# Dense expert layer with choice weights: pacing of the building stretch, place of the weights' second parts, and the buffers of the last activations

## The chip, the cores and the metric

The kernel runs on 1 core of one Trainium2 chip. The metric is device time in microseconds (us), from the first to the last instruction with the launch around it. TensorE (PE), VectorE (DVE), ScalarE (ACT), GpSimd (POOL) and SyncE (SP) each run their own instructions in order and wait for each other by semaphores; DMA transfers are issued from the SP, ACT and POOL queues.

## The reference

Two transformer blocks for 512 tokens of width 1024. The change lies in the expert layer of the first block (PEER), which chooses 16 of 16384 one-neuron experts per token and head:

```python
q = (xb @ wq).reshape(PEER_BLOCK, PEER_HEADS, 2, PEER_DKEY // 2)
s1 = jnp.einsum('thd,hnd->thn', q[:, :, 0], keys[:, 0])
s2 = jnp.einsum('thd,hnd->thn', q[:, :, 1], keys[:, 1])
v1, i1 = lax.top_k(s1, PEER_TOPK)          # the same for s2
...
e = i1[ci // 16] * PEER_NKEYS + i2[ci % 16]
g = jax.nn.softmax(sc, axis=-1)
hid = jnp.einsum('thkd,td->thk', u[e], xb)
a = jax.nn.gelu(hid, approximate=False) * g
return jnp.einsum('thk,thkd->td', a, v[e])
```

Everything is float32.

## The kernel before

Matrix products are made of three float32r products: a weight tile `raw` is split into a first part `whi` (ACT copies and rounds it, L147) and a second part `wlo` (DVE subtracts, L149), and `mm_segs` multiplies both by the first part of the activations (L71, L72) and `whi` by their second part (L76).

The expert layer treats its first 128 tokens by gathered rows and the other 384 densely. **Dense part, first half:** for all 128 groups of 128 experts, `G = gelu(U x)` is computed by `hidden(i)`, a unit of two groups. A unit has two pieces (weight tiles of 512 KB, `raw<-in_peer_u`); a piece has four row tiles, each of six 384-column matmuls, so 24 matmuls. The Gelu (L1262) of a unit comes in the next unit's first step; its result goes from tile `G` (2 buffers) to DRAM (`Gd`, issued on ACT's queue). `wget` splits weights two pieces ahead: at the start of piece i it issues `whi` and `wlo` of piece i+2, with 3 buffers each.

**Beside it runs a side stream**, which `pace` mixes with the units: a unit is cut into `PARTS` main steps, and after each the side stream is given a share of time in units of a written cost table. It holds

- the *choice*: `topk_block` for four blocks of 128 tokens (DVE's max, match and index operations, POOL multiplications);
- the *building* of the dense choice weights A in six chunks of 64 tokens, 16 build steps each. A step issues on DVE the one-hots `o2` (L1212) and `o1` (L1215) of two steps ahead, on ACT four scalings of `o2` (L1214, `hot<-hot`), on PE four matmuls into `aps` (L1232; two PSUM buffers), and on ACT the copy of the step before into `ab` (L1235); `ab` goes to DRAM (`Ad`) by 16 writes, issued one per later step from ACT, those of the last chunk from POOL (L1287) after the side stream;
- the *rows*: for the first 128 tokens, `rg.step` gathers 128 rows of U by an indirect DMA (POOL, L1019, 4 row buffers) and reduces them on DVE (L1028). `UH` = 120 of them are due before the side stream ends, of which `UT` during the choice.

From the start of the building on, DVE and ACT run in the order in which the code is written (`manual_schedule`); PE, POOL and SP are ordered by a scheduler. `N1` groups lie beside the side stream; the units that are left (`i >= N1 // 2`) follow it alone. Then comes the **second half** (peer_v): for each group DVE multiplies `gt` (its G) by `at` (its part of A, read back from `Ad`, L1308), ACT and DVE split the product, and 24 matmuls (L55, L56, L58) accumulate into eight PSUM tiles that `rg.empty` has cleared by eight 512-column matmuls with a zero tile `rz` (L1052, L1054). The second half begins with the last four groups, whose G (units 62 and 63) never goes to DRAM: in the kernel before their Gelu writes tiles `gt` of the pool `lp`, which is opened after the building's pools are closed and takes their memory.

Of the kernel before, what the change touches and what calls it, by code (L numbers as in the profile page):

```python
# [9 lines left out]
F32 = mybir.dt.float32  # L10
F32R = mybir.dt.float32r
# [7 lines left out]
P = 128  # L19
# [26 lines left out]
def r32(ap):  # L46
    return ap.bitcast(F32)
# [17 lines left out]
def mm_segs(nc, x, items, start, stop):  # L65

    xh, xl = x
    for s in range(len(items[0][0])):
        sl = items[0][0][s][1]
        for segs, (lh, ll) in items:  # L70
            nc.tensor.matmul(segs[s][0], lh, xh[:, sl], start=start, stop=False)  # L71
            nc.tensor.matmul(segs[s][0], ll, xh[:, sl], start=False, stop=False)  # L72
    for s in range(len(items[0][0])):
        sl = items[0][0][s][1]
        for segs, (lh, _) in items:
            nc.tensor.matmul(segs[s][0], lh, xl[:, sl], start=False, stop=stop)  # L76


def setup(tc, es, A):
    g = Ctx()  # L80
    nc = tc.nc
    g.tc, g.nc, g.A = tc, nc, A
    g.const = es.enter_context(tc.tile_pool(name="const", bufs=1))
    g.res = es.enter_context(tc.tile_pool(name="res", bufs=1))
    g.wp = es.enter_context(tc.tile_pool(name="wp", bufs=3))
    g.np_ = es.enter_context(tc.tile_pool(name="np", bufs=2))
    c = g.const

    def cin(name, shape, now=True):
        t = c.tile(shape, F32, name="c_" + name)  # L90
        if now:
            nc.sync.dma_start(t, A[name])
        return t

    g.cin = cin
    g.vec = cin("vecs", [P, NVEC])
    g.ident = cin("ident", [P, P], False)
    g.ones = c.tile([P, P], F32, name="ones")
    nc.gpsimd.memset(g.ones, 1.0)
    g.eps = c.tile([P, 1], F32, name="eps")  # L100
    nc.gpsimd.memset(g.eps, EPS)
    g.zero = c.tile([P, 1], F32, name="zero")
    nc.gpsimd.memset(g.zero, 0.0)
    g.pre = {}
    g.raw = {}
    g.nraw, g.third = 0, None
    g.queue = []
    g.h = [None] * KT
    h_tiles(g)
    return g  # L110


def h_tiles(g):
    for k in range(KT):
        g.h[k] = g.res.tile([P, T], F32, tag=f"h{k}", name=f"h{k}")
# [23 lines left out]
    return raw  # L139


def wload(g, raw, pool, hl):

    nc = g.nc
    _, a, b = raw.shape
    hi = pool.tile([P, a, b], F32R, tag="whi", name="whi", bufs=hl)
    nc.scalar.activation(hi, raw, AF.Copy)  # L147
    lo = pool.tile([P, a, b], F32R, tag="wlo", name="wlo", bufs=hl)
    nc.vector.tensor_tensor(lo, raw, r32(hi), op=ALU.subtract)  # L149
    return hi, lo  # L150


def wstart(g, name, *idx):

    key = (name, idx)
    if key not in g.raw and key not in g.pre:
        g.raw[key] = wraw(g, wsrc(g, name, idx))


def wpre(g, name, *idx):  # L160

    key = (name, idx)
    if key not in g.pre:
        wstart(g, name, *idx)
        g.pre[key] = wload(g, g.raw.pop(key), g.wp, 3)


def wget(g, name, *idx):

    key = (name, *idx)  # L170
    wpre(g, *key)
    if key in g.queue[:1]:
        g.queue.pop(0)
        for k in g.queue[:2]:
            wpre(g, *k)
        for k in g.queue[2:3 if g.third is None else 4]:
            wstart(g, *k)
    return g.pre.pop((name, idx))


def gemm_fm(g, segs, name, ct, rhs):
# [10 lines left out]
def gemm2(g, accs, name, ct, rhs, out=None, pieces=None):  # L192

    keys = keys2(g, name, ct, pieces)
    for i, key in enumerate(keys):
        hi, lo = wget(g, *key)
        for k in range(4):
            ws = [(hi[:, k, e * P:(e + 1) * P], lo[:, k, e * P:(e + 1) * P]) for e in range(2)]
            mm_segs(g.nc, rhs(4 * i + k), list(zip(accs, ws)), i == 0 and k == 0, i == len(keys) - 1 and k == 3)
            yield 1.3  # L200
    if out is not None:
        out()
# [734 lines left out]
NK = 128  # L937
# [2 lines left out]
LAST = 3  # L940

AHEAD_V = 2
N1 = 122
PARTS = 4


GT = 128
# [5 lines left out]
CH = 64  # L953
NCK = ND // CH

UH, UT = 120, 44

T16, T256, TLK, BUILD, ROW = 2.2, 3.1, 2.0, 1.3, 1.4
TOPKS = 16 * T16 + 3 + 8 * T256 + 8 * TLK + 2
# [101 lines left out]
def peer_block(g, ni, tail):  # L1061

    tc, nc, A = g.tc, g.nc, g.A
    with ExitStack() as es:
# [14 lines left out]
        with ExitStack() as e1:  # L1079
# [161 lines left out]
                for i in range(0, NK, n):  # L1241
                    out.append((Ad[c, :, i:i + n], buf[:, i:i + n]))

            def hidden(i, ts=None):

                at = {}

                def step(p):
                    if p == 0:
                        at["acc"] = [acc.get(ND) for _ in range(2)]  # L1250
                        at["gen"] = gemm2(g, [a[0] for a in at["acc"]], "peer_u", i, X)
                    for _ in range(8 // PARTS):
                        next(at["gen"])
                    if p == 0 and ends:
                        ends.pop(0)()
                    if p == PARTS - 1:
                        ends.append(end)

                def end():
                    gt = gp.tile([P, 2, ND], F32, tag="G", name="G") if ts is None else ts  # L1260
                    for e in range(2):
                        nc.scalar.activation(gt[:, e], at["acc"][e][1], AF.Gelu)  # L1262
                    if ts is None:
                        nc.scalar.dma_start(Gd[i], gt)
                return [(lambda p=p: step(p)) for p in range(PARTS)]

            ends = []
            chosen, picked = {}, {}
            out = []

            def weights():

                for b in range(4):
                    for n, c in enumerate(topk_block(b)):
                        yield c
                        if n == 12 and GT < b * P:
                            chosen[b - 1] = tokens_last(b - 1)
                for _ in range(8):
                    yield 1.0
                chosen[3] = tokens_last(3)  # L1280
                order_kept.append(kept.enter_context(tc.manual_schedule(engines={mybir.EngineType.DVE, mybir.EngineType.Activation})))
                e2.close()
                ab = e1.enter_context(tc.tile_pool(name="p_ab", bufs=2))
                for c in range(NCK):
                    yield from build(ab, c)
                while out:
                    tc.keep_in_program_order(nc.gpsimd.dma_start(*out.pop(0)))  # L1287
# [23 lines left out]
        def two_in(i):  # L1311

            gt = lp.tile([P, 2, ND], F32, tag="gt", name="gt", bufs=3)
            if i < NK - FIRST:
                tc.keep_in_program_order(nc.scalar.dma_start(gt, Gd[i // 2]))
            return gt


        ats, gts = {}, {}

        def expert(n):
            i = order[n]
# [16 lines left out]
            return lo  # L1339

        ats[NK - FIRST] = four_in(NK - FIRST)
        for i in range(NK - FIRST, NK, 2):
            gts[i] = two_in(i)

        for i in range(N1 // 2, NK // 2):
            for m in hidden(i, gts.get(2 * i)):
                m()
        while ends:
            ends.pop(0)()
        h_tiles(g)  # L1350
        tail.load(es)
        accs = [pp.tile([P, 512], F32, name=f"acc{k}") for k in range(3)] + [acc.get()[1] for _ in range(5)]
# [923 lines left out]
```

## Time and profile before

| | |
|---|---|
| device time, median of 3 runs | 3642.78 us (3641.7 to 3643.01) |
| the profiled execution's own time | 3628.02 us |
| its span | 3626.3 us |
| PE busy in the span | 3483.1 us (96%) |
| DVE busy | 2399.4 us (66%) |
| ACT busy | 1591.4 us (44%) |
| POOL busy | 776.2 us (21%) |
| mean granted TensorE clock | 0.981 |

The profile is of one execution. Matmuls are pipelined, so PE's busy time overstates its work; what is read below is mostly idle time ahead of an instruction, with what ended it. In rows of the trace, a line is that of the kernel before, "x" counts instructions, and a bracket gives the idle time of the engine just before and the releaser.

### The profile page before, as it was taken

The numbers are of one execution on the slowest core, as the hardware profiler recorded it, in microseconds if no ns is written. First come the engines' busy times: TensorE is split into PE (matmuls) and PEld (weight loads), VectorE is DVE, ScalarE is ACT, GpSimd is POOL, SyncE is SP. The second block draws the span as 40 slices with busy tenths as digits, with TensorE's granted clock in tenths as the row PEclk, the third lists the DMA queues.
The fourth block names the chain that finished last, engine by engine and source line by source line (L and its number), as shares of the span: only waits on it lengthen the run. The fifth ranks groups of instructions, "written<-read, shape, count | busy, mean of one in ns | idle before, by whom it ended". The sixth has DMA issues, their size and how long they took to land. (4 is left out here: it accounts for less than half of the span.)

```text
span 3626.3 us, 56462 instructions
## 1 busy us (share of the span) xinstructions
PE 3483.1 (96%) x21979; PEld 3164.9 (87%) x21979; DVE 2399.4 (66%) x4395; ACT 1591.4 (44%) x2998; POOL 776.2 (21%) x828
## 2 busy tenths in 40 slices
PE   8999999999898889999999999999999999999999
PEld 6777888898887779999998899999899998878887
DVE  5764457999967658888887677767643345564433
ACT  4555333333477763333346444445422235343222
POOL 2421010333322232333332322222100003120000
PEclk9999999999999999999998999999999999999999
DMA  4233233566678889999972121111132322213222
GB/s 134 76 88 88 82 124 122 198 225 221 233 237 279 270 299 369 358 360 353 363 257 77 56 63 57 47 52 52 48 98 90 94 88 83 75 59 99 93 93 93
DMA packets 169492, 557.60 MB, mean 154 GB/s; under 512 B 19617, under 2 KB 20130, under 8 KB 169224
## 3 DMA queue, kind: packets, MB, share of 16 engines
q1 hardware_dynamic: 90228, 313.50, 26.1%
q0 software_dynamic: 49136, 170.64, 14.2%
q10 hardware_dynamic: 29860, 69.84, 5.3%
q8 instruction: 173, 2.83, 0.3%
q14 instruction: 95, 0.78, 0.1%
HBM read 492.20 MB, written 55.41 MB: 151 GB/s over the span
## 5 line engine op out<-in xcount | busy, mean ns | idle before, releaser
L72 PE MATMUL ps<-xh,wlo 128*128 128x264 f32 (+2 forms) x3296 | 1051.3, 331 | 45.0 <-DVE wlo L149 44.8
L71 PE MATMUL ps<-xh,whi 128*128 128x264 f32 (+2 forms) x3296 | 1069.6, 337 | 18.8 <-ACT xh L288 13.5
L149 DVE TENSOR_TENSOR wlo<-raw,whi 128x1024 fp32r<-128x1024 f32 x562 | 718.6, 1279 | 531.2 <-ACT whi L147 524.8
L147 ACT ACTIVATE whi<-raw 128x1024 fp32r<-128x1024 f32 x562 | 594.5, 1058 | 978.9 <-PE ps L76 782.6
L76 PE MATMUL ps<-xl,whi 128*128 128x264 f32 (+2 forms) x3296 | 813.1, 331 | 6.5 <-DVE xl L289 6.4
L72 PEld LDWEIGHTS ps<-xh,wlo 128*128 128x128 f32 x3296 | 629.6, 192 | 91.5 <-DVE wlo L149 61.4
L71 PEld LDWEIGHTS ps<-xh,whi 128*128 128x128 f32 x3296 | 630.2, 192 | 59.3 <-ACT xh L288 15.9
L76 PEld LDWEIGHTS ps<-xl,whi 128*128 128x128 f32 x3296 | 563.6, 192 | 39.3 <-DVE xl L289 8.9
L1019 POOL DMA_INDIRECT row<-in_peer_ur_dram,rix x128 | 146.1, 1142 | 465.7 <-DVE row L1028 372.1
L71 PE MATMUL ps<-ah,whi 128*128 128x264 f32 (+1 forms) x768 | 230.1, 320 | 0.0
L72 PE MATMUL ps<-ah,wlo 128*128 128x264 f32 (+1 forms) x768 | 229.9, 320 | 0.0
L55 PE MATMUL ps<-ah,whi 128*128 128x384 f32 x640 | 215.5, 337 | 0.0
L56 PE MATMUL ps<-ah,wlo 128*128 128x384 f32 x640 | 215.1, 336 | 0.0
L1019 POOL DMA_INDIRECT row<-in_peer_v_dram,rix x128 | 138.1, 1079 | 276.9 <-DVE ro L1032 261.5
L280 POOL TENSOR_TENSOR ssum<-ssum,sq 128x512 f32<-128x512 f32 (+1 forms) x49 | 75.1, 1538 | 460.4 <-ACT sq L279 459.8
L1028 DVE SCALAR_TENSOR_TENSOR row<-row,rx 128x1024 f32<-128x1024 f32 x128 | 164.0, 1283 | 6.2 <-DMA row<-in_peer_ur_dram,rix 6.2
L1333 ACT ACTIVATE ah<-gt 128x384 fp32r<-128x384 f32 x128 | 67.3, 526 | 227.4 <-DVE gt L1331 227.4
L76 PE MATMUL ps<-al,whi 128*128 128x264 f32 (+1 forms) x768 | 163.2, 321 | 0.0
L1214 ACT ACTIVATE hot<-hot,lt 128x128 f32<-128x128 f32 x384 | 122.0, 390 | 93.3 <-DVE hot L1212 89.6
L1032 DVE SCALAR_TENSOR_TENSOR ro<-row,rhid,ro 128x1024 f32<-128x1024 f32 x127 | 162.4, 1278 | 0.6 <-DMA row<-in_peer_v_dram,rix 0.4
L71 PEld LDWEIGHTS ps<-ah,whi 128*128 128x128 f32 x768 | 144.3, 188 | 11.4
L72 PEld LDWEIGHTS ps<-ah,wlo 128*128 128x128 f32 x768 | 144.3, 188 | 10.9
(429 smaller groups left out, 6184.7 us busy)
## 6 DMA issues: line engine op xcount, KB each, us to landing
raw<-in_peer_u_dram SPq DMA_DIRECT2D x128, 512.0 KB, 5.5
raw<-in_peer_v_dram SPq DMA_DIRECT2D x128, 512.0 KB, 6.9
raw<-in_ff_up_dram SPq DMA_DIRECT2D x64, 512.0 KB, 3.4
raw<-in_ff_down_dram SPq DMA_DIRECT2D x64, 512.0 KB, 3.5
at<-Ad POOLq DMA_DIRECT2D x32, 768.0 KB, 7.2
raw<-in_gdn_in_dram SPq DMA_DIRECT2D x48, 512.0 KB, 3.5
Gd<-G ACTq DMA_DIRECT2D x62, 384.0 KB, 3.2
gt<-Gd ACTq DMA_DIRECT2D x62, 384.0 KB, 5.2
```

The lines of the kernel that those rows point to most:

```text
L55: nc.tensor.matmul(out, lh, rh, start=start, stop=False)
L56: nc.tensor.matmul(out, ll, rh, start=False, stop=False)
L71: nc.tensor.matmul(segs[s][0], lh, xh[:, sl], start=start, stop=False)
L72: nc.tensor.matmul(segs[s][0], ll, xh[:, sl], start=False, stop=False)
L76: nc.tensor.matmul(segs[s][0], lh, xl[:, sl], start=False, stop=stop)
L147: nc.scalar.activation(hi, raw, AF.Copy)
L149: nc.vector.tensor_tensor(lo, raw, r32(hi), op=ALU.subtract)
L280: g.nc.gpsimd.tensor_tensor(self.t[:, 0:n], self.t[:, 0:n], sq[:, 0:n], op=ALU.add)
L1019: nc.gpsimd.indirect_dma_start(out=t, out_offset=None, in_=(self.U, self.V)[e], in_offset=bass.IndirectOffsetOnAxis(ap=self.ix[:, j:j + 1] ...
L1028: o = nc.vector.scalar_tensor_tensor(t, t, 1.0, self.x, op0=ALU.mult, op1=ALU.mult, accum_out=a)
L1032: o = nc.vector.scalar_tensor_tensor(self.o, t, a, self.o, op0=ALU.mult, op1=ALU.add)
L1214: nc.scalar.activation(oh[:, j], o2[:, j], AF.Copy, scale=lt[:, 2, 4 * t4 + j:4 * t4 + j + 1])
```

## The change

Five edits. (1) From the start of the building to the end of the first half (`g.late`), `wload` returns a function that makes `wlo`; `gemm2` calls it after the matmuls of the first row tile of the piece that is being multiplied. (2) `PARTS` 4 to 8: a main step is one row tile, not two, and the side stream's share per step is halved. (3) `N1` 122 to 118: ten groups (five units) are left behind the side stream, not six (three units); as the share per step is the side stream's cost over `N1`, it grows by 122/118. (4) `UT` 44 to 28: fewer rows during the choice, more during the building. (5) The Gelu of units 62 and 63 writes tiles `G` of the pool `gp`, from which the second half reads; `lp`'s three `gt` buffers hold loaded groups alone.

```diff
-def wload(g, raw, pool, hl):
+def wload(g, raw, pool, hl, late=False):
...
     nc.scalar.activation(hi, raw, AF.Copy)
-    lo = pool.tile([P, a, b], F32R, tag="wlo", name="wlo", bufs=hl)
-    nc.vector.tensor_tensor(lo, raw, r32(hi), op=ALU.subtract)
-    return hi, lo
+
+    def second():
+        lo = pool.tile([P, a, b], F32R, tag="wlo", name="wlo", bufs=hl)
+        nc.vector.tensor_tensor(lo, raw, r32(hi), op=ALU.subtract)
+        return hi, lo
+    if late:
+        return second
+    return second()
...
+    wsecond(g, (name, idx))
     return g.pre.pop((name, idx))
+
+def wsecond(g, *keys):
+    for key in keys or list(g.pre):
+        if callable(g.pre[key]):
+            g.pre[key] = g.pre[key]()
...
             mm_segs(g.nc, rhs(4 * i + k), list(zip(accs, ws)), i == 0 and k == 0, i == len(keys) - 1 and k == 3)
+            if k == 0:
+                wsecond(g)
             yield 1.3
...
-N1 = 122
-PARTS = 4
+N1 = 118
+PARTS = 8
...
-UH, UT = 120, 44
+UH, UT = 120, 28
...
-                    gt = gp.tile([P, 2, ND], F32, tag="G", name="G") if ts is None else ts
+                    gt = gp.tile([P, 2, ND], F32, tag="G", name="G")
                     for e in range(2):
                         nc.scalar.activation(gt[:, e], at["acc"][e][1], AF.Gelu)
-                    if ts is None:
+                    if 2 * i < NK - FIRST:
                         nc.scalar.dma_start(Gd[i], gt)
+                    else:
+                        gts[2 * i] = gt
...
                 order_kept.append(kept.enter_context(tc.manual_schedule(engines={mybir.EngineType.DVE, mybir.EngineType.Activation})))
+                g.late = True
...
         for i in range(N1 // 2, NK // 2):
-            for m in hidden(i, gts.get(2 * i)):
+            for m in hidden(i):
                 m()
         while ends:
             ends.pop(0)()
+        g.late = False
```

What the change moves in the instruction order, counted over the whole order of PE and DVE:

| | before | now |
|---|---|---|
| pieces of U on PE ahead of the first `aps` | 77 | 70 |
| pieces on PE behind the last `aps` | 4.9 | 8.9 |
| DVE, choice: `wlo` / row reductions, from the first max of the choice to the first `o2` of the building proper | 76 / 46 | 69 / 30 |
| DVE, building: pieces with build steps between their `wlo` and the next | 43 | 44 |
| of their `wlo`, row reductions right behind it, ahead of the next `o2` | 21 | 15 |
| DVE, building: pieces with two row reductions and no build step behind them (the last piece of the building left out) | 1 | 3 |
| DVE, building: build steps' one-hots | 93 | 93 |

DVE in the building, before (`hot<-iota`: L1212 is `o2`, L1215 `o1`; `row` is a row reduction):

```order
L149 TENSOR_TENSOR wlo<-raw,whi 128x1024
L1028 SCALAR_TENSOR_TENSOR row,rhid<-row,rx 128x1024
L1212 TENSOR_TENSOR hot<-iota,lt_7977 128x512
L1215 TENSOR_TENSOR hot<-iota,lt_7977 128x512
L1028 SCALAR_TENSOR_TENSOR row,rhid<-row,rx 128x1024
L1212 TENSOR_TENSOR hot<-iota,lt_7977 128x512
L1215 TENSOR_TENSOR hot<-iota,lt_7977 128x512
L149 TENSOR_TENSOR wlo<-raw,whi 128x1024
```

The same engine in the building of the changed kernel (L151 is `wlo`, L1227 `o2`, L1230 `o1`, L1043 a row reduction):

```order
L151 TENSOR_TENSOR wlo<-raw,whi 128x1024
L1227 TENSOR_TENSOR hot<-iota,lt_7773 128x512
L1230 TENSOR_TENSOR hot<-iota,lt_7773 128x512
L1043 SCALAR_TENSOR_TENSOR row,rhid<-row,rx 128x1024
L1227 TENSOR_TENSOR hot<-iota,lt_7773 128x512
L1230 TENSOR_TENSOR hot<-iota,lt_7773 128x512
L1043 SCALAR_TENSOR_TENSOR row,rhid<-row,rx 128x1024
L151 TENSOR_TENSOR wlo<-raw,whi 128x1024
```

Two build steps lie between two `wlo` in both; a row reduction has moved from ahead of the first one-hot to behind the second.

ACT at the same two pieces, before (their `whi`, and what lies between; `hot<-hot` is the scaling of `o2`, `ab<-aps` the copy of a build step):

```order
L147 ACTIVATE whi<-raw 128x1024
L1214 ACTIVATE hot<-hot,lt_7977 128x128 x4
L1235 ACTIVATE ab<-aps 128x4x128
L1237 DMA Ad<-ab 128x512
L1214 ACTIVATE hot<-hot,lt_7977 128x128 x4
L1235 ACTIVATE ab<-aps 128x4x128
L1237 DMA Ad<-ab 128x512
L147 ACTIVATE whi<-raw 128x1024
```

And ACT in the changed kernel, between the `whi` of the two pieces whose `wlo` are shown for it:

```order
L147 ACTIVATE whi<-raw 128x1024
L1229 ACTIVATE hot<-hot,lt_7773 128x128 x4
L1250 ACTIVATE ab<-aps 128x4x128
L1252 DMA Ad<-ab 128x512
L1229 ACTIVATE hot<-hot,lt_7773 128x128 x4
L1250 ACTIVATE ab<-aps 128x4x128
L1252 DMA Ad<-ab 128x512
L147 ACTIVATE whi<-raw 128x1024
```

Between two `whi` on ACT stand the scalings of as many build steps as one-hots stand between the matching `wlo` on DVE, before and now; this holds for every piece of the building proper.

ACT at the join of the two halves in the changed kernel (L1277 Gelu; `whi` here are the last pieces of U and the first of peer_v):

```order
L1277 ACTIVATE G<-ps 128x384 x2
L1279 DMA Gd_4666<-G 128x768
L147 ACTIVATE whi<-raw 128x1024 x2
L1277 ACTIVATE G<-ps 128x384 x2
L147 ACTIVATE whi<-raw 128x1024
L1277 ACTIVATE G<-ps 128x384 x2
L1067 ACTIVATE rz<-rpair 128x128
L1351 ACTIVATE ah<-G 128x384
```

The order is that of the kernel before; there the last two Gelus write `gt` in place of `G`.

## Rows read from the trace of the kernel before

**Rows 1.** Busy us by stretch: PE, PEld, DVE, ACT, POOL, clock, DMA share, GB/s

```profile
600.00:976.00 376.00, 347.69 (x1928) 335.64 (x1927) 361.59 (x1001) 135.10 (x198) 121.79 (x70) 0.96 0.64 209
976.00:1329.00 353.00, 311.55 (x1887) 280.07 (x1886) 253.55 (x381) 264.29 (x559) 82.24 (x75) 0.99 0.82 265
1329.00:1361.00 32.00, 23.77 (x123) 22.16 (x122) 8.72 (x9) 9.51 (x16) 16.36 (x28) 0.89 0.90 331
```

**Rows 2.** Groups of DVE, 600 to 976: busy us, mean ns, idle before, releasers

```profile
L149 DVE TENSOR_TENSOR wlo<-raw,whi 128x1024 fp32r<-128x1024 f32 x75 | 109.0, 1455 | 1.5 <-ACT whi L147 1.4
L1028 DVE SCALAR_TENSOR_TENSOR row<-row,rx 128x1024 f32<-128x1024 f32 x46 | 64.4, 1399 | 6.2 <-DMA row<-in_peer_ur_dram,rix 6.2
```

**Rows 3.** Groups of PE, 600 to 976

```profile
L72 PE MATMUL ps<-xh,wlo 128*128 128x384 f32 x600 | 208.1, 347 | 28.3 <-DVE wlo L149 28.1
```

**Rows 4.** Groups of DVE, 976 to 1329

```profile
L149 DVE TENSOR_TENSOR wlo<-raw,whi 128x1024 fp32r<-128x1024 f32 x45 | 55.1, 1225 | 98.8 <-ACT whi L147 95.5 <-DMA Ad<-ab 3.2
```

**Rows 5.** Groups of ACT, 976 to 1329

```profile
L1214 ACT ACTIVATE hot<-hot,lt 128x128 f32<-128x128 f32 x372 | 118.1, 390 | 86.1 <-DVE hot L1212 82.4 <-PE ps L76 1.1
```

**Rows 6.** Groups of PE, 976 to 1329

```profile
L1232 PE MATMUL aps<-hot 128*128 128x128 f32 x768 | 108.9, 284 | 24.2 <-ACT ab L1235 22.7
```

**Rows 7.** Timeline of DVE in the building: start us, us, instruction, idle before

```profile
1104.91 1.23 DVE L149 TENSOR_TENSOR wlo<-raw,whi 128x1024 fp32r<-128x1024 f32 x1 [2.57 <-ACT whi L147]
1106.05 1.22 DVE L1028 SCALAR_TENSOR_TENSOR row<-row,rx 128x1024 f32<-128x1024 f32 x1
...
1107.19 0.68 DVE L1212 TENSOR_TENSOR hot<-iota,lt 128x512 f32<-128x512 f32 x1
...
1113.39 1.23 DVE L149 TENSOR_TENSOR wlo<-raw,whi 128x1024 fp32r<-128x1024 f32 x1 [2.56 <-ACT whi L147]
...
1120.82 1.23 DVE L149 TENSOR_TENSOR wlo<-raw,whi 128x1024 fp32r<-128x1024 f32 x1 [1.50 <-ACT whi L147]
...
1128.21 1.23 DVE L149 TENSOR_TENSOR wlo<-raw,whi 128x1024 fp32r<-128x1024 f32 x1 [2.62 <-ACT whi L147]
...
1135.63 1.23 DVE L149 TENSOR_TENSOR wlo<-raw,whi 128x1024 fp32r<-128x1024 f32 x1 [1.50 <-ACT whi L147]
...
1144.98 1.23 DVE L149 TENSOR_TENSOR wlo<-raw,whi 128x1024 fp32r<-128x1024 f32 x1 [3.23 <-ACT whi L147]
...
1149.07 1.23 DVE L149 TENSOR_TENSOR wlo<-raw,whi 128x1024 fp32r<-128x1024 f32 x1 [0.57 <-ACT whi L147]
```

**Rows 8.** Timeline of ACT in the building

```profile
1107.97 0.40 ACT L1214 ACTIVATE hot<-hot,lt 128x128 f32<-128x128 f32 x1 [3.10 <-DVE hot L1212]
```

**Rows 9.** Timeline of DVE in the second half: first and last of five

```profile
1374.05 1.23 DVE L149 TENSOR_TENSOR wlo<-raw,whi 128x1024 fp32r<-128x1024 f32 x1 [0.90 <-ACT whi L147]
...
1390.69 1.23 DVE L149 TENSOR_TENSOR wlo<-raw,whi 128x1024 fp32r<-128x1024 f32 x1 [0.24 <-ACT whi L147]
```

**Rows 10.** Timeline of PE at the join

```profile
1347.61 0.51 PE L76 MATMUL ps<-xl,whi 128*128 128x384 f32 x2
1355.76 1.65 PE L1054 MATMUL acc<-xh,rz 128*128 128x512 f32 x3 [7.64 <-ACT rz L1052]
...
1360.12 0.44 PE L55 MATMUL acc<-ah,whi 128*128 128x384 f32 x1 [0.59 <-ACT ah L1333]
```

**Rows 11.** Timeline of ACT at the join

```profile
1352.93 0.87 ACT L1262 ACTIVATE gt<-ps 128x384 f32<-128x384 f32 x2 [10.02 <-DMA row<-in_peer_ur_dram,rix]
...
1355.38 0.33 ACT L1052 ACTIVATE rz<-rpair 128x128 fp32r<-128x128 f32 x1
```

**Rows 12.** Timeline of POOL at the join

```profile
1344.57 0.54 POOL L1287 DMA_DIRECT2D Ad<-ab x1 [0.28 <-DMA Ad<-ab]
...
1353.50 0.88 POOL L1308 DMA_DIRECT2D at<-Ad x1 [6.65 <-issue]
```

**Rows 13.** DMA issues, 976 to 1329: KB each, median us to landing

```profile
Gd<-G ACTq DMA_DIRECT2D x22, 384.0 KB, 3.0
row<-in_peer_ur_dram,rix POOLq DMA_INDIRECT x75, 5.7
```

More of the change, by code (lines that the diff above doesn't have):

```diff
@@ L105, in setup @@
     g.raw = {}
-    g.nraw, g.third = 0, None
+    g.nraw, g.third, g.late = 0, None, False
     g.queue = []
@@ L164, in wpre @@
         wstart(g, name, *idx)
-        g.pre[key] = wload(g, g.raw.pop(key), g.wp, 3)
+        g.pre[key] = wload(g, g.raw.pop(key), g.wp, 3, g.late)
 def wget(g, name, *idx):
@@ L1242, in build, with hidden @@
                     out.append((Ad[c, :, i:i + n], buf[:, i:i + n]))
-            def hidden(i, ts=None):
+            def hidden(i):
                 at = {}
@@ L1268, in peer_block @@
             chosen, picked = {}, {}
+            gts = {}
             out = []
@@ L1313, in two_in @@
             gt = lp.tile([P, 2, ND], F32, tag="gt", name="gt", bufs=3)
-            if i < NK - FIRST:
-                tc.keep_in_program_order(nc.scalar.dma_start(gt, Gd[i // 2]))
+            tc.keep_in_program_order(nc.scalar.dma_start(gt, Gd[i // 2]))
             return gt
-        ats, gts = {}, {}
+        ats = {}
         def expert(n):
@@ L1341, in peer_block @@
         ats[NK - FIRST] = four_in(NK - FIRST)
-        for i in range(NK - FIRST, NK, 2):
-            gts[i] = two_in(i)
         for i in range(N1 // 2, NK // 2):
-            for m in hidden(i, gts.get(2 * i)):
+            for m in hidden(i):
                 m()
```

## The prediction

> **What bounds the kernel now.** I read the three stretches in which the change lies, first as a table of busy time [rows 1]. In the choice (600 to 976 us) DVE is busy 361.59 of 376 us and PE 347.69. In the building (976 to 1329) no engine is full: PE 311.55, ACT 264.29, DVE 253.55 of 353. At the join (1329 to 1361) PE works 23.77 of 32.
>
> The groups with their idle times say who waits for whom. In the choice PE loses 28.3 us, all of it ahead of matmuls with `wlo` [rows 3], while DVE waits for ACT only 1.5 us ahead of `wlo` [rows 2]: DVE sets the pace, and PE is 8% short of it. In the building the waits form a ring: DVE stands 98.8 us ahead of `wlo`, for `whi` on ACT [rows 4]; ACT stands 86.1 us ahead of the scalings, for the one-hots on DVE [rows 5]; PE stands 24.2 us ahead of `aps`, for the copies on ACT [rows 6]. One turn in the timeline shows the ring. DVE starts `wlo` at 1104.91 when `whi` is done, a row reduction at 1106.05, the next one-hot at 1107.19 [rows 7]; only then can ACT scale, at 1107.97 after 3.10 us of idling [rows 8]; ACT then does both build steps and the next `whi`, and DVE, long done with its one-hots, waits 2.56 us for that until 1113.39 [rows 7].
>
> So a turn has a price by what lies between two `wlo`, and the starts in [rows 7], read with the order of DVE there, give it. Two build steps with a row reduction ahead of the first one-hot: 1104.91 to 1113.39, 8.48 us. Two without: 7.43, 7.39 and 7.42 us, of which the first and third have a row reduction behind the last one-hot, where it costs nothing because DVE waits there anyway. Three build steps without: 9.35 us. Two row reductions and no build step: 4.09 us. Hence 1.95 us for a build step (9.35 - 7.40), 3.50 for the piece itself (7.40 - 2 x 1.95), 1.08 for a row reduction ahead of the first one-hot. PE needs less than a turn: 24 matmuls take 4.16 us (1374.05 to 1390.69 in four pieces [rows 9]) and a build step 1.13 (108.9 us over 96 steps [rows 6]), 6.4 together.
>
> **The second parts behind the first row tile: nothing.** DVE runs in written order here. The call stands ahead of the generator's `yield`, so no side work comes between: in the order shown, the same number of one-hots stands between two `wlo` as scalings between the two `whi`. `wlo` still blocks all DVE work behind it. The edit adds no instruction and moves none on DVE or ACT, so no cover can be lost with it.
>
> **Choice: -28.** DVE has 7 `wlo` and 16 row reductions fewer ahead of the building. By their starts either holds DVE 1.14 us (1104.91 to 1106.05 to 1107.19 [rows 7]): 23 x 1.14 = 26.2, the lower bound. By their means in this stretch, 1.455 and 1.399 us [rows 2], it is 10.2 + 22.4 = 32.6, the upper bound; there GpSimd's multiplications hold some of them up, and these stay whatever they hit. PE has 7 pieces fewer, 7 x 4.16 = 29.1, so it doesn't become the bound. I take 28, nearer to the undisturbed price since most of them are undisturbed. The Trainium skill (page "GPSIMD Engine Reference", section "8. Key points") says that GpSimd shares its SBUF interfaces with VectorE and contends with DVE instructions that have two SBUF inputs, as both of these have; the longer means beside a busy POOL agree. Read so that every removed operation takes its share of the contention along, the rule speaks for the upper bound, and the whole sum would be 4.6 us lower.
>
> **Building: +5.** The turns are counted from the order. Before: 43 x 3.50 + 21 x 1.08 + 93 x 1.95 + 1 x 4.09 = 358.7, against a stretch of 353 [rows 1]; it is over because at chunk borders copies run beside pieces without one-hots, and there are five borders before and now. Now: 44 x 3.50 + 15 x 1.08 + 93 x 1.95 + 3 x 4.09 = 363.9. So the 16 moved row reductions cost nothing (fewer stand ahead of a first one-hot), the finer main steps give 6.5 us by that, and three more pieces cost 11.7. Bounds: if the two added pieces without build steps run beside border copies, -3; if each costs a whole turn of 7.40, +12.
>
> **Tail: +16.6.** Four more pieces follow the last `aps`; they run at PE's own pace, 4 x 4.16. This is certain unless their weights come late (below).
>
> **Join: -8.7.** PE's last matmul of U ends at 1348.12, the first of the second half starts at 1360.12 [rows 10]. Of these 12.0 us the eight clearing matmuls would need 8 x 0.23 = 1.8 at the pace of [rows 9] (4.16 / 24 for 384 columns, by 512/384); 10.2 are lost. The chain: the Gelu of unit 62 stands 10.02 us to 1352.93 [rows 11], and the read of A is issued at 1353.50 after 6.65 us [rows 12]. Both end together, after the last write of `Ad` (issued 1344.57): the Gelu because its tile lies in the building's memory, the read because it needs the data. The trace names a row gather as releaser of the Gelu; the memory is my reading. Then come the second Gelu (0.87), `rz` (0.33 [rows 11]), the clearing. With the Gelus in `G` the first wait goes. With 16.6 us more of matmuls behind the last write, the read of A, which ended ahead of 1360, ends before PE needs it. Left are the last Gelu, `rz` and hand-overs, about 1.5 us, since `rz` still stands behind that Gelu on ACT: 10.2 - 1.5 = 8.7. Bounds: -10.2 (all), -4 (the writes land late). The `G` buffer itself is free in time: its write to `Gd` was issued two units (16.6 us) earlier and lands in 3.0 us [rows 13].
>
> **Sum.** -28 + 5 + 16.6 - 8.7 = **-15.1 us**. The profiled execution took 3628.02 us (span 3626.3), 14.8 below the median of the runs, so its sum is 3612.9; from the median 3642.78 I predict **3627.7 us**. Counted the other way, in PE's idle time: choice +1 (29.1 of work gone, 28 of time), building 5 - 3 x 4.16 = -7.5, join -8.7; the same -15.
>
> **Rivals.** (B) *Each term at its better end*: -32.6 - 3 + 16.6 - 10.2 = -29.2, 3613.6 us. The busy POOL in the choice speaks for it; that PE itself would need 29.1 less there speaks against more. (C) *The tail's loads collide with the last writes*: at the join the DMA share is 0.90 already [rows 1], and now four more 512 KB pieces and two more `Gd` writes are moved beside the 16 writes of `Ad`. The Trainium skill (page "DMA: Bandwidth & Descriptors", section "Issuing engines are not separate DMA queues") says that DMAs of all issuing engines run on the same 16 engines and interleave, which would make both later. If the writes end 8 us later the join gives 2 instead of 8.7, and with PE waiting one piece, 4.2, in the tail the sum is -4.2: 3638.6 us, no change that can be told. Against it: the tail is 37 us long now, and the writes were done 24 us after the building's end. (D) *Row gathers become late in the building*: 93 row reductions in some 358 us are one in 3.85 us, and with four buffers a gather has three of these, 11.5 us, for issue and landing. Landing takes 5.7 us [rows 13]; if the higher load doubled it, each row reduction would take a third of the landing time: at 12.5 us, 93 x 4.17 = 388, 30 us more than the ring, and the sum is +15, 3658 us. It decides from 11.5 us on. For it: the DMA share of 0.82 [rows 1] gets 17 gathers more. Against it: in the building DVE's idle time is accounted for by `whi` alone [rows 4]. (E) *The second parts do come free of the ring*: a turn would fall to PE's 6.4 us, 44 x 1.0 = 44 us off the sum, 3584 us. The order shown speaks against it.
>
> **How the numbers follow.** Forecast 0.50 (its own range 3620 to 3635), B 0.13, C and other poor ends of the bounds 0.23, D 0.11, E 0.03. About 0.2%, 7.3 us, is what a measurement of this kernel can tell from no change: faster (below 3635.5) are the forecast, B and E, 0.66; the same C, 0.23; slower D, 0.11. The range 3614 to 3643 takes in B to C with the poor ends (-24 + 12 + 16.6 - 4 = +0.6) and leaves out D, E and little more.
>
> **What would show it.** Right: the choice some 28 us shorter with DVE still full; in the building DVE still waiting about 90 us for `whi` ahead of `wlo`, turns of 7.4 and 8.5 us, a length near 358; PE running without a gap from the last `aps` for 37 us, then idle about 1.5 us, with the granted clock kept. Wrong: `wlo` without a wait (E), row reductions waiting for a DMA (D), idle PE of over 4 us at the join or matmuls in the tail waiting for `whi` (C).

## The result and the profile after

The changed kernel takes **3620.82 us** (median of 8 runs, 3612.04 to 3626.59) against 3642.87 for the kernel before beside it: ratio **0.9943** (95% interval 0.9925 to 0.9961), 22 us less. The forecast was 3627.7 us. The profiled execution (span 3621.0) shows where the 22 us come from.

Rows of the changed kernel by stretch, columns as in [rows 1]:

```profile
600.00:945.00 345.00, 316.27 (x1749) 305.58 (x1749) 322.73 (x953) 123.36 (x181) 99.30 (x53) 0.97 0.57 189
945.00:1302.00 357.00, 323.01 (x1954) 289.53 (x1953) 275.10 (x417) 268.81 (x565) 99.37 (x91) 1.00 0.87 290
1302.00:1342.00 40.00, 39.01 (x222) 38.34 (x221) 14.90 (x16) 17.10 (x27) 17.30 (x28) 1.00 0.97 367
```

The stretches are cut at the first `aps`, the last, and the first matmul of the second half: choice, building, tail with join. The marks are in the trace by tile (first and last start, ahead of the semicolon): the last of four blocks' `lists` ends the choice on DVE, the first and last `aps` bound the building on PE. First the kernel before, then the changed one:

```profile
L1178 DVE TENSOR_TENSOR lists<-w,z x4: 281/292/292, 672.3 to 970.7; 128x128 f32<-128x128 f32 x4
L1232 PE MATMUL aps<-hot x768: 270/275/378, 976.1 to 1327.3; 128*128 128x128 f32 x192
...
L1193 DVE TENSOR_TENSOR lists<-w,z x4: 285/290/291, 669.9 to 939.5; 128x128 f32<-128x128 f32 x4
L1247 PE MATMUL aps<-hot x768: 270/275/378, 945.5 to 1301.5; 128*128 128x128 f32 x192
```

Read in the same way for every kernel (starts, us from the span's start; "between" is from the first to the last `aps`; "call" is the call that makes `wlo`, described with the experiments):

| kernel | last `lists` | first `aps` | last `aps` | between | first matmul of the second half |
|---|---|---|---|---|---|
| before | 970.7 | 976.1 | 1327.3 | 351.2 | 1360.1 |
| changed | 939.5 | 945.5 | 1301.5 | 356.0 | 1342.0 |
| G buffers alone | 971.1 | 977.4 | 1329.3 | 351.9 | 1363.6 |
| N1 alone | 961.5 | 968.0 | 1310.7 | 342.7 | 1351.1 |
| N1 and G | 960.2 | 967.4 | 1309.9 | 342.5 | 1350.4 |
| UT alone | 947.5 | 952.5 | 1323.1 | 370.6 | 1356.3 |
| changed, PARTS = 4 | 942.2 | 946.2 | 1302.3 | 356.1 | 1342.8 |
| changed, call at second tile | 940.6 | 947.1 | 1261.2 | 314.1 | 1301.7 |
| changed, call at third tile | 941.2 | 945.6 | 1255.0 | 309.4 | 1295.5 |
| before, call at second tile | 970.1 | 976.3 | 1327.8 | 351.5 | 1360.2 |
| before, call at third tile | 968.6 | 974.3 | 1268.9 | 294.6 | 1302.6 |
| before, call at third tile, and N1 | 961.9 | 967.6 | 1259.4 | 291.8 | 1299.8 |
| changed, call at second tile, build step's cost 0.8 | 953.6 | 963.8 | 1272.9 | 309.1 | 1313.4 |
| changed, call at second tile, build step's cost 0.6 | 959.6 | 971.9 | 1269.1 | 297.2 | 1309.0 |

So the choice, up to the first `aps`, gave 30.6 us (forecast 28), the building took 4.8 more (forecast 5), tail and join took 7.7 more (40.5 in place of 32.8; forecast 16.6 - 8.7 = 7.9): 18.1 us less at the first matmul of the second half, 15.1 forecast. At the end of the two profiled executions only 5.3 are left, while the medians differ by 22: the profile of before is of an execution 14.8 us below its median, that of after 1.9 above (3622.76). The stages behind are the same program in both, and of their drift nothing is made here: even one order of instructions drifts there. The kernel before and the run "before, call at second tile", in which all rows stand as in the kernel before, are 0.1 us apart at this mark and 18.3 at the end (spans 3626.3 and 3644.6).

The groups of the changed kernel, first DVE and PE in the choice (600 to 945), then DVE, ACT and PE in the building (945 to 1302):

```profile
L151 DVE TENSOR_TENSOR wlo<-raw,whi 128x1024 fp32r<-128x1024 f32 x68 | 90.4, 1329 | 0.2 <-ACT whi L147 0.2
L1043 DVE SCALAR_TENSOR_TENSOR row<-row,rx 128x1024 f32<-128x1024 f32 x29 | 46.3, 1597 | 4.8 <-DMA row<-in_peer_ur_dram,rix 4.8
L1174 DVE TENSOR_REDUCE lists<-cand 128x64 f32<-128x1024 f32 x16 | 19.4, 1212 | 10.5 <-POOL cand L1171 10.5
L72 PE MATMUL ps<-xh,wlo 128*128 128x384 f32 x544 | 188.7, 347 | 28.7 <-DVE wlo L151 28.5
...
L151 DVE TENSOR_TENSOR wlo<-raw,whi 128x1024 fp32r<-128x1024 f32 x48 | 58.8, 1225 | 82.1 <-ACT whi L147 50.8 <-ACT ab L1250 31.3
L1043 DVE SCALAR_TENSOR_TENSOR row<-row,rx 128x1024 f32<-128x1024 f32 x92 | 111.7, 1219 | 0.0
L1229 ACT ACTIVATE hot<-hot,lt 128x128 f32<-128x128 f32 x372 | 118.4, 390 | 86.3 <-DVE hot L1227 78.3 <-PE ps L76 5.1 <-issue 0.3
L72 PE MATMUL ps<-xh,wlo 128*128 128x384 f32 x394 | 132.0, 350 | 16.4 <-DVE wlo L151 16.4
L1247 PE MATMUL aps<-hot 128*128 128x128 f32 x768 | 109.7, 285 | 17.1 <-ACT ab L1250 15.4
```

The ring is where it was. DVE stands 82.1 us ahead of `wlo` (98.8 in [rows 4]), ACT 86.3 ahead of the scalings (86.1 in [rows 5]); PE still loses 28.7 us in the choice for want of `wlo` (28.3 in [rows 3]). The releaser "ACT ab" is the copy that stands beside `whi` in ACT's order. The starts of `wlo` in DVE's timeline are 7.42 us apart, as three of the turns in [rows 7] were:

```profile
1108.30 1.22 DVE L151 TENSOR_TENSOR wlo<-raw,whi 128x1024 fp32r<-128x1024 f32 x1 [1.48 <-ACT whi L147]
...
1115.72 1.23 DVE L151 TENSOR_TENSOR wlo<-raw,whi 128x1024 fp32r<-128x1024 f32 x1 [1.50 <-ACT ab L1250]
...
1123.14 1.23 DVE L151 TENSOR_TENSOR wlo<-raw,whi 128x1024 fp32r<-128x1024 f32 x1 [1.49 <-ACT ab L1250]
```

The join of the changed kernel, timelines of PE, ACT and POOL:

```profile
1340.00 0.97 PE L1069 MATMUL acc<-xh,rz 128*128 128x512 f32 x3 [0.99 <-ACT rz L1067]
1340.81 1.33 PE L1069 MATMUL ps<-xh,rz 128*128 128x512 f32 x5
1341.98 0.34 PE L55 MATMUL acc<-ah,whi 128*128 128x384 f32 x1
...
1338.88 0.87 ACT L1277 ACTIVATE G<-ps 128x384 f32<-128x384 f32 x2 [2.94 <-PE ps L76]
...
1331.64 0.88 POOL L1327 DMA_DIRECT2D at<-Ad  x1 [8.80 <-DMA raw<-in_peer_v_dram]
```

PE's idle 7.64 us of [rows 10] are 0.99; the Gelu waits for PE's matmuls and no longer for its tile [rows 11]; the read of A is issued 10 us ahead of its use, where before it was issued 5.4 us behind PE's last matmul of U [rows 12].

### The profile page after: what moved, and what is told of

Its sections match the earlier page's. It is cut to its first block, busy times and chain, and to the rows that moved or that the text cites. A ratio compares the mean times of both kernels' runs of the same rounds, so it can differ in the third digit from the quotient of the medians.

```text
span 3621.0 us, 56455 instructions
## 1 busy us (share of the span) xinstructions
PE 3493.1 (96%) x21979; PEld 3175.1 (88%) x21979; DVE 2390.1 (66%) x4395; ACT 1592.1 (44%) x2998; POOL 771.0 (21%) x828
## 5 line engine op out<-in xcount | busy, mean ns | idle before, releaser
L151 DVE TENSOR_TENSOR wlo<-raw,whi 128x1024 fp32r<-128x1024 f32 x562 | 709.7, 1263 | 512.9 <-ACT whi L147 476.2
L72 PEld LDWEIGHTS ps<-xh,wlo 128*128 128x128 f32 x3296 | 631.8, 193 | 90.4 <-DVE wlo L151 60.3
L1043 DVE SCALAR_TENSOR_TENSOR row<-row,rx 128x1024 f32<-128x1024 f32 x128 | 166.5, 1305 | 4.8 <-DMA row<-in_peer_ur_dram,rix 4.8
L1047 DVE SCALAR_TENSOR_TENSOR ro<-row,rhid,ro 128x1024 f32<-128x1024 f32 x127 | 162.5, 1280 | 4.4 <-DMA row<-in_peer_v_dram,rix 4.2
L72 PEld LDWEIGHTS ps<-ah,wlo 128*128 128x128 f32 x768 | 144.3, 188 | 10.9
```

The costliest lines, as they stand in the source:

```text
L1043: o = nc.vector.scalar_tensor_tensor(t, t, 1.0, self.x, op0=ALU.mult, op1=ALU.mult, accum_out=a)
L1047: o = nc.vector.scalar_tensor_tensor(self.o, t, a, self.o, op0=ALU.mult, op1=ALU.add)
```

## The experiments

**G buffers alone.** Kernel before, with the last Gelus' output in `G`:

```diff
-                    gt = gp.tile([P, 2, ND], F32, tag="G", name="G") if ts is None else ts
+                    gt = gp.tile([P, 2, ND], F32, tag="G", name="G")
...
-                    if ts is None:
+                    if 2 * i < NK - FIRST:
                         nc.scalar.dma_start(Gd[i], gt)
+                    else:
+                        gts[2 * i] = gt
```

> Kernel before with one part of the change: the last Gelus go into G buffers, their groups are written to Gd and read back. Theory of the prediction: at the join two waits end together, the Gelu's for its buffer and the read of A behind the last write of Ad; taking away the first alone leaves the second, so PE's first matmul of the second half stays within 1.5 us of its old distance from the last aps (32.8 us), and the time is the same as before (0 us, within 0.2%). Rival (the buffers are what the join's gain is made of): the Gelu runs about 10 us earlier and PE with it, -8 to -10 us at the join, 24 us from the last aps to the first expert matmul.

Measured: 3647.54 us, 1.0013 of before (0.9999 to 1.0027). Timelines of PE and POOL at the join:

```profile
1351.05 0.97 PE L1054 MATMUL acc<-xh,rz 128*128 128x512 f32 x3 [0.99 <-ACT rz L1052]
...
1363.56 0.69 PE L55 MATMUL acc<-ah,whi 128*128 128x384 f32 x1 [10.38 <-ACT ah L1335]
...
1357.21 0.88 POOL L1311 DMA_DIRECT2D at<-Ad  x1 [6.72 <-DMA raw<-in_peer_v_dram]
```

The Gelu and with it the clearing run early, then PE stands 10.38 us for `ah`, which is made of the product with `at`; the read of `at` is issued at 1357.21. So the wait has moved behind the clearing: 34.3 us from last `aps` to the second half instead of 32.8. The theory holds. That it is the last write of `Ad` which holds the read back stays a reading of the program; the trace names another transfer (`raw`).

**N1 alone.** `N1 = 122` to `118`, last Gelus still in `gt`.

> Kernel before with N1 = 118 alone: two more units (four more pieces) in the tail, the last Gelus still in the building's memory. By the order the choice loses 5 second weight parts and 1 row reduction, 6 x 1.14 = 6.8 us; the building has 41 pieces, 20 of its row reductions ahead of a first one-hot: 356.7 by the turn prices against 358.7, -2 us; the tail has 16.6 us more matmuls. Theory: these matmuls cover the last writes of Ad, the read of A and the Gelu's wait for its buffer, without any G buffer, so the join loses about 1.5 us only (-8.7) and the distance from last aps to first expert matmul is 32.8 + 7.9 = 40.7 us; the sum is -1 us. Rival (the buffers are needed): the Gelu's wait stays, the distance is 49 us, the sum +8 us.

Measured: 3632.33 us, 0.9979 (0.9969 to 0.999), -7.6. Timelines of PE and ACT:

```profile
1349.13 0.96 PE L1054 MATMUL acc<-xh,rz 128*128 128x512 f32 x3 [0.99 <-ACT rz L1052]
...
1348.01 0.49 ACT L1262 ACTIVATE gt<-ps 128x384 f32<-128x384 f32 x1 [2.94 <-PE ps L76]
```

The longer tail covers both waits with the old tile `gt`; from last `aps` to the second half are 40.4 us (40.7 expected). At the second half it is 9.0 us ahead of before where 1 was expected; most of the miss is in the building, 8.5 us shorter where the turn prices give 2, and why is not shown.

**N1 and G.** Both edits above together.

> Kernel before with N1 = 118 and the G buffers. N1 = 118 alone ran at 0.998 of the time before, with PE idle for only 0.99 us at the join. Theory: with the longer tail the Gelu's wait for its old buffer is covered anyway, so the G buffers add nothing: the time of N1 = 118 alone (3632 us, within 0.2%), PE idle about 1 us at the join. Rival (the buffers give a part of the gain of the change also there): 4 us or more below N1 = 118 alone.

Measured: 3632.55 us, 0.998 (0.9968 to 0.9992), PE idle 0.99 us at the join. The buffers add nothing.

**UT alone.** `UT = 44` to `28`.

> Kernel before with UT = 28 alone. By the order the choice has 4 second weight parts and 15 row reductions fewer, 19 x 1.14 = 21.7 us; the building has 45 pieces, 21 row reductions ahead of a first one-hot and three pieces without a build step: 45 x 3.50 + 21 x 1.08 + 93 x 1.95 + 3 x 4.09 = 373.8 against 358.7, +15 us; tail and join as before. Theory (turn prices are right, ring of DVE and ACT paces the building): last `lists` of the choice about 22 us earlier, first to last aps about 366 us, sum -6.6 us. Rival (row reductions moved into the building are free, since DVE waits there for whi anyway, and pieces cost only what PE needs): the building grows by 2 x 4.2 = 8 us at most, the sum is -13 us; that would say that the smaller UT is the whole gain of the change.

Measured: 3640.62 us, 1.0005 (0.9987 to 1.0023); 3.8 us earlier at the second half. First `aps` 23.6 us earlier (21.7 expected), building 19.4 longer (15 expected, 8 at most by the rival): moving rows into the building isn't free, and the rival falls.

**Changed kernel with PARTS = 4.**

> Changed kernel with PARTS = 4 in place of 8. By the order DVE's instructions from the choice to the join stand as in the changed kernel, row for row; only where PE's matmuls and side work alternate could differ. Theory: no difference to the changed kernel, 3621 us within 0.2%, first to last aps 356 us. Rival (finer main steps spare PE waits between pieces, as the prediction credited them with 6.5 us): 6 us or more slower than the changed kernel, 362 us from first to last aps.

Measured: 3620.64 us, 0.9951 (0.9938 to 0.9964), all marks within 3 us of the changed kernel's. (The expectation's "row for row" holds for the building; in the choice some rows stand elsewhere.) So the finer main steps give nothing.

**Really deferred, in the changed kernel.** In the order of the changed kernel the deferral is no deferral: with `g.late` left False, DVE, ACT and PE have the same rows in the same order (that kernel wasn't run). `whi` of piece i+2 is issued at the start of piece i, the call follows behind the first row tile's matmuls, and the generator's `yield`, at which a main step can end and side work come in, only behind that. Two kernels put the call at the start of the second (`k == 1`) and of the third row tile (`k == 2`):

```diff
+            if k == 1:
+                wsecond(g)
             mm_segs(g.nc, rhs(4 * i + k), ...
-            if k == 0:
-                wsecond(g)
             yield 1.3
```

> Changed kernel, with the second weight parts placed behind a step of the side work: the call stands at the start of the second row tile, so that the generator's yield lies between whi and wlo. Compared with the changed kernel as it is. Theory: in the building DVE's wait for whi ahead of wlo (about 90 us) is the ring's link; once the one-hots of the next step stand ahead of wlo in DVE's order, ACT scales without waiting, a turn falls from 7.4 us towards the 6.4 that PE needs, first to last aps 356 minus 25 to 40 us, and the time is 25 to 40 us below the changed kernel's. Rival: ACT itself (copies, scalings and whi of a turn with their hand-overs) or PE's waits ahead of aps set the pace, and the wait only moves to another instruction: first to last aps 350 to 358, the time the same as the changed kernel's.

> Changed kernel, with the second weight parts at the start of the third row tile, behind two steps of the side work (behind one step: 3578 us, first to last aps 314 us, where 49.25 pieces x 4.16 + 96 x 1.13 = 313 is what PE needs). Theory: once wlo stands behind any one-hots the ring is cut and PE paces the building, so a second step changes nothing: 3578 us within 0.3%, first to last aps 312 to 318. Rival (the later second part reaches PE too late, since it is wanted at the next piece): idle time of PE ahead of matmuls with wlo grows from 6 us to 20 or more, 3590 us or more.

DVE's order in the building, the changed kernel (-) and with the call at the second tile (+):

```
 L1043 SCALAR_TENSOR_TENSOR row,rhid<-row,rx 128x1024
-L151 TENSOR_TENSOR wlo<-raw,whi 128x1024
 L1227 TENSOR_TENSOR hot<-iota,lt_6959 128x512
 L1230 TENSOR_TENSOR hot<-iota,lt_6959 128x512
+L151 TENSOR_TENSOR wlo<-raw,whi 128x1024
```

Measured: 3577.99 us, 0.9832 (0.9814 to 0.985), and 3578.27 us, 0.9833 (0.9819 to 0.9847): 43 us below the changed kernel (40 by the ratios; 40.3 and 46.5 by the marks at the second half), where 25 to 40 were expected of the first. Of the first, two turns in DVE's timeline:

```profile
1109.35 1.22 DVE L151 TENSOR_TENSOR wlo<-raw,whi 128x1024 fp32r<-128x1024 f32 x1
...
1115.56 1.22 DVE L151 TENSOR_TENSOR wlo<-raw,whi 128x1024 fp32r<-128x1024 f32 x1 [0.29 <-issue]
...
1121.79 1.23 DVE L151 TENSOR_TENSOR wlo<-raw,whi 128x1024 fp32r<-128x1024 f32 x1 [0.31 <-issue]
```

Its groups of DVE, ACT and PE in the building, 947 to 1262:

```profile
L151 DVE TENSOR_TENSOR wlo<-raw,whi 128x1024 fp32r<-128x1024 f32 x48 | 58.8, 1224 | 35.4 <-ACT whi L147 20.6 <-ACT ab L1250 10.4 <-issue 4.0
...
L1229 ACT ACTIVATE hot<-hot,lt 128x128 f32<-128x128 f32 x372 | 117.6, 390 | 45.6 <-DVE hot L1227 36.3 <-ACT G L1277 5.4 <-PE aps L1247 2.4
...
L72 PE MATMUL ps<-xh,wlo 128*128 128x384 f32 x394 | 129.2, 342 | 6.3 <-DVE wlo L151 6.3
...
L1247 PE MATMUL aps<-hot 128*128 128x128 f32 x768 | 104.9, 280 | 3.3 <-ACT ab L1250 2.0
```

And the busy time of that stretch, columns as in [rows 1]:

```profile
947.00:1262.00 315.00, 305.37 (x1953) 289.95 (x1952) 274.79 (x415) 266.52 (x565) 101.54 (x91) 1.00 0.93 326
```

A turn takes 6.2 us in place of 7.42; PE waits 9.6 us ahead of its groups in place of 33.5 (16.4 + 17.1) and is busy 305 of 315 us: PE now paces most of the building. The edit only moves `wlo` behind work on which ACT waits. The theory holds and its rival falls, but the ring is loosened rather than gone: ACT still stands 45.6 us ahead of the scalings (86.3 in the changed kernel), DVE 35.4 ahead of `wlo` (82.1). A second step brings nothing that a time shows; by the marks it brings 6.2 us at the second half, 4.7 of them in the building (309.4 us, 312 to 318 expected).

**The deferral alone, on the kernel before.** First with the call at the second row tile, then at the third (the same edits of `wload`, `wget` and `g.late`; N1, UT, PARTS and the Gelus as before).

> Kernel before with one part alone: second weight parts deferred, but placed at the start of the second row tile, behind a step of the side work; N1, UT, PARTS and the join as before. Theory (the wait for whi ahead of wlo was the link of the ring; without it PE is full between first and last aps): 46.25 pieces x 4.16 + 96 build steps x 1.13 = 301 us there instead of 351, so -46 to -50 us in all, about 3593 us. Rival (the deferral pays only together with the shorter choice and fewer row reductions ahead of a first one-hot, 21 here): less than half of that, 3615 us or more.

> Kernel before with the deferral alone, at the start of the third row tile. With PARTS = 4 a main step is two row tiles, and side work comes only between main steps: the same call at the second row tile left every row of DVE, ACT and PE where it was (1.001 of the time before), at the third one-hots come between whi and wlo; ACT's order stays. N1, UT, PARTS and the join as before. Theory (the wait for whi ahead of wlo is the ring's link, whatever N1 and UT are): first to last aps 46.25 pieces x 4.16 + 105 to 109 for the build steps = 297 to 301 us in place of 351, the time -45 to -54 us, 3587 to 3597. Rival (it pays only with the change's other parts): 3615 us or more.

The first: 3644.2 us, 1.001 (0.9999 to 1.0021). The expectation was wrong: with `PARTS` 4 a main step is two row tiles, so no side work comes between the first and the second, and all rows of DVE, ACT and PE stand as in the kernel before. It is thus a measurement of no change, and its marks agree with those of before within 0.6 us. The second: 3580.87 us, **0.9837** (0.9811 to 0.9862), -61 (-45 to -54 expected). Its PE groups from 974 to 1270:

```profile
L72 PE MATMUL ps<-xh,wlo 128*128 128x384 f32 x371 | 122.6, 344 | 5.4 <-DVE wlo L151 5.2
...
L1247 PE MATMUL aps<-hot 128*128 128x128 f32 x768 | 102.9, 276 | 2.6 <-ACT ab L1250 2.2
```

And PE's timeline at the join:

```profile
1298.04 1.65 PE L1069 MATMUL acc<-xh,rz 128*128 128x512 f32 x3 [8.28 <-ACT rz L1067]
```

294.6 us between first and last `aps`, 56.6 fewer than before (50 to 54 expected): one moved call gives about three times what the whole change gives, without any of its other parts. The wait for `whi` was the link that held the building back.

**The deferral with N1.**

> Kernel before with two parts: the deferral at the start of the third row tile (alone 3581 us, PE idle 8.3 us at the join) and N1 = 118. Theory: the longer tail covers the join (8 us less idle), and 2.5 pieces fewer ahead of the first aps leave PE some 3 us more idle in the choice; first expert matmul at about 1298 us instead of 1302.6, the time 3576 us. UT = 28, PARTS = 8 and the G buffers would then be worth nothing measurable beside these two (all together with a real deferral: 3578 us). Rival (UT or the buffers are needed with it): 3586 us or more, or PE idle over 4 us at the join.

Measured: 3583.69 us (3576 expected), 0.9834 (0.9809 to 0.9859), PE idle 0.99 us at the join, second half at 1299.8 us (1298 expected). The join's wait is gone, but the time can't be told from the deferral alone, nor from the changed kernel's parts with it: beside a real deferral, N1, UT, PARTS and G are worth nothing that a time shows, and by the marks 7 us at most (1295.5 against 1302.6), to which come some 2 us behind the mark, where the lower clock after the join's gap still holds PE up (last section).

**More pieces in the choice**, to use PE's idle time there (25.5 us with the call at the second tile). Changed kernel, call at the second tile, `BUILD = 1.3` to `0.8` and `0.6`.

> Changed kernel with the second parts at the second row tile (3578 us) and a cost of 0.8 in place of 1.3 for a build step in the pacing. By the order the choice has 2 second parts more and 2 row reductions fewer, PE 76.25 pieces instead of 70 ahead of the first aps and 43 instead of 49.25 between first and last. Theory: PE's idle time in the choice (25.5 us ahead of matmuls with wlo) is what can still be won; two more pieces fit there at no DVE time, so -8 us: 3570; first to last aps about 43 x 4.16 + 105 = 284. Rival (ACT, which needs some 290 us for its work between first and last aps, or DVE paces the building as soon as PE has less to do there): first to last aps 295 or more, and no gain: 3578 within 0.2%, or above.

> As the run with a cost of 0.8, with 0.6: 4 second parts more and 1 row reduction fewer in the choice than at 1.3 (3 x 1.14 = 3.4 us of DVE), 78.75 pieces ahead of the first aps, 40.6 between first and last, which PE needs 274 us for. Theory: 4 pieces, 16.6 us, for 3.4 us, -13 us against 3578: 3565. Rival (ACT or DVE paces the building): first to last aps 290 or more, 3575 us or above.

Measured: 3597.06 us, 0.9872 (0.9846 to 0.9898), and 3587.44, 0.9859 (0.9829 to 0.9889): neither is faster than with 1.3 (0.9832); the second half comes 11.7 and 7.3 us later. Of the first, PE's and DVE's groups from 960 to 1280:

```profile
L72 PE MATMUL ps<-xh,wlo 128*128 128x384 f32 x363 | 120.5, 347 | 12.9 <-DVE wlo L151 12.7
L1247 PE MATMUL aps<-hot 128*128 128x128 f32 x768 | 106.7, 282 | 9.0 <-ACT ab L1250 7.5 <-ACT hot L1229 0.2
...
L151 DVE TENSOR_TENSOR wlo<-raw,whi 128x1024 fp32r<-128x1024 f32 x46 | 56.3, 1225 | 43.2 <-ACT whi L147 27.4 <-ACT ab L1250 13.3 <-issue 2.5
```

The first `aps` came 16.7 us later, not at the same time. The expected counts don't fit the trace: from 670 us to the last `lists` DVE's trace has 58 `wlo` against 53 with 1.3 and 28 row reductions in both, not two more and two fewer; DVE is busy 15.6 us longer there (268.9 against 253.3), and the choice takes 13.0 longer. So more pieces in the choice cost DVE time. The building took 309 us where its pieces were estimated to need PE for 284: PE stands 21.9 us ahead of the two groups shown (9.6 with 1.3), so with fewer pieces beside the same build steps it no longer paces the stretch. That the second kernel, with still fewer pieces, reaches the second half 4.4 us ahead of the first stays unexplained.

## Why the prediction was right

*Second parts: 0.* Right: on the kernel before, a call that moves no row gave 1.001 and marks within 0.6 us. The case that the prediction set aside as E (they come free of the ring, 44 us at 0.03) needed an order that the change doesn't have; the call one row tile later gives that order, and 43 us (40 by the marks).

*Choice: -28.* Measured -30.6, right in size, but partly by luck. DVE's busy time in `wlo` and row reductions fell by 36.7 us (109.0 + 64.4 in [rows 2] to 90.4 + 46.3), more than the upper bound 32.6 (these windows hold 17 row reductions fewer, not 16); but DVE now waits 10.5 us ahead of `lists` for POOL's `cand`, where before it was this row's 3.8:

```profile
L1159 DVE TENSOR_REDUCE lists<-cand 128x64 f32<-128x1024 f32 x16 | 19.3, 1209 | 3.8 <-POOL cand L1156 3.8
```

36.7 - 6.7 = 30.0. (Over all its instructions DVE is busy 38.9 us less and idle 7.9 more.) The prediction set the relief too low and left out the wait that came back, and the two nearly cancel. That a busier DVE had covered POOL is a reading of these rows. The Trainium skill (page "GPSIMD Engine Reference", section "8. Key points") says that DVE instructions with two SBUF inputs contend with GpSimd for its shared interfaces. The prediction's other reading of this, that every removed operation takes its share of the contention along, comes near the 36.7 in sum, but not by operation (7 `wlo` took 18.6 us along; 17 row reductions took 18.1, 1.06 each, less than the undisturbed 1.14), and not for the time of the stretch.

*Building: +5.* Measured +4.8, but one reason given for it was wrong: "the finer main steps give 6.5 us by that". The 15 row reductions ahead of a first one-hot stand there with `PARTS` 4 too, and the building takes 356.1 us. They come from N1 and UT together: by the order N1 alone leaves 20 and UT alone 21; they change the building by -8.5 and +19.4, 10.9 in sum, where the changed kernel has 4.8. Five fewer than 20, at 1.08 us, are 5.4 of the difference of 6.1. The turn prices held to 6.5 us at worst (N1 alone).

*Tail and join: +7.9.* Measured +7.7. That two waits end together at the join was right. But the tail alone hides both; "with the Gelus in `G` the first wait goes" is true and worth nothing, alone (+1.5 us from last `aps` on) or beside the longer tail (0). Of rival C the loads were late indeed (ACT stands 1.3 to 3.5 us for `raw` ahead of seven `whi` of the tail), but no matmul of the tail waited for them: PE is busy 39.01 of the 40 us.

*Sum.* At the second half 18.1 us against 15.1; the time came out 7 us below the forecast, within the range. Three of the 7 us stand at that mark; the rest can't be told, as the interval of the ratio allows a gain of 14 to 27 us. N1 alone gives 9.0 us at that mark and UT alone 3.8; the 5.3 left are covered by their interaction in the building, 6.1. D (late row gathers) did not come: ahead of DVE's row reductions in the building the changed kernel shows no idle time (0.0 in the groups above). Two slips of the working change nothing: the counts of turns add up to 358.6 and 363.8, with the same difference, and the upper end of the range takes the choice at -24 where its lower bound was 26.2, which would give 3641 in place of 3643.

## What to carry to other kernels

Where two in-order engines wait for each other in turns, look in the order for the instruction that waits for the other engine's newest result, and move it behind work that the other engine will need next; here its own consumer was two pieces away. Check that the moved call is really past a point where other work is mixed in: here the same call was worth nothing at one row tile, and 43 to 61 us one row tile later. And when a stall has two causes that end together, take both away or lengthen the cover: here a longer cover hid both, and taking one away alone gave nothing.

## What the runs showed of the hardware

The granted clock after idle time shows in the clearing matmuls and those behind them. Stretches of the kernel before, then of the deferral alone (call at third tile), columns as in [rows 1]:

```profile
1356.00:1360.00 4.00, 3.54 (x8) 2.23 (x8) 0.56 (x2) 0.45 (x1) 2.97 (x7) 0.53 0.85 290
1360.00:1364.00 4.00, 3.88 (x22) 3.88 (x23) 2.86 (x5) 1.54 (x3) 0.52 (x1) 1.00 0.86 270
...
1298.00:1302.00 4.00, 3.78 (x8) 2.48 (x8) 0.84 (x2) 0.01 (x1) 2.93 (x6) 0.50 0.86 287
1302.00:1306.00 4.00, 3.43 (x11) 3.43 (x12) 2.41 (x4) 1.99 (x3) 0.97 (x2) 0.50 0.80 240
```

In the kernel before, after 7.64 us of idle, the clearing ran at 0.53, near the lower level of 1.2 GHz: 512 columns took 628 ns. From 1360 on the clock was 1.00. In the changed kernel, after 0.99 us, it was 1.00 and 512 columns took 398 ns. With the deferral alone, after 8.28 us, it was 0.50 up to 1306, and the first matmuls of the second half took 522 ns in place of 336: clearing and the first 24 matmuls took 3.8 and 6.6 us, against 2.0 and 4.2 in the changed kernel, so 4 us beyond the gap itself. That is no fixed price. In the kernel before only the clearing was slow; and the run in which all rows stand as in the kernel before (call at second tile) had 0.50 up to 1364 after 7.37 us of idle, with matmuls of 522 ns.

One order of instructions, measured twice (kernel before, and the deferral that moves nothing), gave 1.001; and the kernel before alone had medians from 3640.08 to 3645.81 us in its five measurements. Differences of 0.1 to 0.2% are therefore read here from the marks, and from a time only where its interval leaves out 1.

The mean of an instruction in a contended stretch didn't carry over: in the choice `wlo` fell from 1455 to 1329 ns while row reductions rose from 1399 to 1597. Which operations lie beside POOL's in either kernel was not counted.
